# An encoder layer on one core: one loop over the feature groups for both requests, activations streamed from DRAM, f16 output projection

## The chip, the cores and the metric

One core of a Trainium2 chip runs the whole kernel in one launch. The metric is the device time of that launch in microseconds; lower is better.

## The reference, cut to what matters

Two requests, a prompt of 2048 tokens ("p") and a sample of 512 ("s"), go through one layer with the same weights:

```python
shift, scale, gate = split(silu(c) @ w_ada + b_ada, 3)
h = rmsnorm(x, g_pre) * (1 + scale) + shift
[qa ka va ga | qb kb vb gb] = h @ w_in          # 1024 -> 4096
ya = dilated_mixture(rope(qa), rope(ka), va) * silu(ga)   # 8 heads, windows (128,1) (512,4) (2048,16)
yb = diff_attention(rope(qb), rope(kb), vb) * silu(gb)    # 4 heads, two softmax maps, dense over the request
y = concat(ya, yb) @ w_out                      # 1024 -> 1024
out = x + gate * rmsnorm(y, g_post)
```

Everything is float32 with a tight tolerance, so each float32 product is made of three f16 products of a high and a low half (high by high, high by low, low by high); in the output projection the halves are of the 32-bit type that the trace shows as f32.

## The kernel before, in words

The 1024 mixed features are eight groups of 128: groups 4 to 7 are the four heads of B, groups 0 to 3 are four pairs of heads of A. Tokens are taken in superblocks of 512: the prompt has four, the sample one. For a group and a superblock there are four pieces of work: `kv_proj` (L421, matmuls in L433), `qg_proj` (queries in L508, gate in L529), the attention items (`ItemB`, L549, or `ItemA`, L661), and the write of the result to DRAM (L654, L757). A group of B has four items in a superblock, a group of A eight.

An item of B makes scores (L571, L577) in PSUM, a maximum on VectorE (L579), its negative on GpSimd (L582), the exponential on ScalarE (L587), the difference of the two maps and its high and low halves (L604, L606, L614), turns these by DMA transposes (L607, L615) and multiplies with the values (L626). An item of A makes scores of two kinds: for the two wide windows in four 32-column groups of the array (L681), and for the narrow window with all 128 columns at once (L686). For that second form `qg_proj` copies the queries of A into another order (L538). It then adds masks, takes maxima (L691, L693), exponentials (L700), halves (L715, L717), transposes (L718, L719), and multiplies (L735, L741).

**Order of the work.** `units` (L902) is a list of 16: first the sample with the eight groups in `ORDER` (4, 0, 5, 1, 6, 2, 7, 3), then the prompt with the same eight. The loop at L928 goes over units and over their superblocks. In each turn `interleave` (L884) mixes the attention items ("main") with projections that are needed next ("fill"), by estimated costs; the tile framework then places the instructions on the engines' queues in an order of its own, by a model of time. Queues are in order. All DMAs, transposes among them, are issued by SyncE (SP).

In the sample's eight units the weights of a group are loaded (`raw_load`, L160), scaled by their largest entry (`raw_split`, L257: L264 and a reduction over partitions on GpSimd, L272), split into halves (L286, L287), used, and also written to DRAM (L289). The prompt's units load the halves from there (`load_w`, L291). In the sample's last units the prompt's activations h are made too (`make_h`, L343); all four superblocks then stay in SBUF. PSUM is dealt out anew at L930: while the sample is worked on, scores are 512 wide in 3 banks, 3 banks for projections, 2 for the rest; after it three score tiles of two banks each, one bank for projections, one for the rest.

The output projection (`out_proj`, L819) reads y of one 128-token tile, splits it (L827, L829), makes 48 matmuls of 512 columns (L845), a mean square (L850), and adds x (L852, L853). There are 20 tiles; 16 are given as fill to the last superblock of the last unit, with a factor of 0.1 on their cost (`LF`, L997) that puts nearly all of them behind it, 4 come after (L999).

Of the kernel before, what the change touches and what calls it, by code (L numbers as in the profile page):

```python
# [8 lines left out]
F32 = mybir.dt.float32  # L9
# [19 lines left out]
LF = 0.1  # L29
PPB, HLB, ATB, SCB, PJB, PVB = 5, 4, 3, 3, 1, 1  # L30
PSI = 0
SSC, SPJ, SPV = 3, 3, 2
HSU = ((0,), (), (1,), (2,), (3,))
AQ = 1
WOA = [4, 1]
# [6 lines left out]
def hybrid_kernel(ctx, tc, x_p, x_s, w_in, w_ada, w_out, cvec, cols, lamv, gsub,  # L42
# [11 lines left out]
    CPM = SMAX // 4 + 32  # L54
# [11 lines left out]
    wp = stack_wp.enter_context(tc.tile_pool(name="wp", bufs=3))  # L66
# [3 lines left out]
    def psum(sw, sc, pj, pv):  # L70
        """deal the banks of PSUM out to scores (sw floats wide), projections and the rest"""
# [10 lines left out]
    psum(512, SSC, SPJ, SPV)  # L82
# [29 lines left out]
    cols_sb = C([P, 42], F32, "cols")        # b_ada, g_pre, g_post, feature 128 k + p at [p, k]; row sums  # L112
# [11 lines left out]
    # DRAM scratch  # L124
    w_spill = {g: dr.tile([P, 2, KT, 2, 256], F16, tag=f"wsp{g}", name=f"wsp{g}") for g in range(8)}
# [25 lines left out]
    def pow2(e_out, inv_out, src, name):  # L151
        """e_out: the power of two at or below src (>= 1e-30); inv_out: 2 / e_out."""
# [4 lines left out]

    RAW = {}

    def raw_load(n):  # L160
        raw = T(big, [P, KT, 512], F32, f"hT{1 + n % 2}")
        nc.sync.dma_start(raw, w_in[ORDER[n]])
        RAW[n] = raw

# [12 lines left out]
    def ada(ps, wa, scp, b0):  # L177
        """ps[:, b0 + q, :] = 128 columns of silu(c) @ w_ada on the partitions, from 512 columns wa of w_ada"""
# [13 lines left out]
    def modulation():  # L192
# [3 lines left out]
        for n, slot in enumerate(("hT2", "hT3", None, "hT0")):  # L196
            if slot:
                t = T(big, [P, KT, 512], F32, slot)
                halves = t[:, 0:4], t[:, 4:8]
            else:  # L200
                halves = [T(kv, [P, KT // 2, 512], F32, "K") for _ in range(2)]
# [8 lines left out]
        for r in "sp":  # L210
# [8 lines left out]
            g3 = T(tn, [P, 2], F32, "g3")  # L219
            nc.gpsimd.partition_all_reduce(g3, g2, channels=P, reduce_op=bass.bass_isa.ReduceOp.max)  # L220
            G = T(tn, [P, 1], F32, "G")
            V.tensor_add(G, g3[:, 0:1], g3[:, 1:2])
            E = T(tn, [P, 1], F32, "E")
            S = T(tn, [P, 1], F32, "S")
            pow2(E, S, G, f"h{r}")
# [5 lines left out]
    gcol = C([P, KT, 2], F32, "gcol")        # gate * g_post  # L231

    def gate_half(n):
        wa = T(big, [P, KT, 512], F32, "hT3")
# [22 lines left out]
    def raw_split(n):  # L257
        """Scale and split w_in of the n-th group; keep a copy of the halves in DRAM."""
        g, raw = ORDER[n], RAW[n]
        mg = T(tn, [P, 1], F32, "mg")  # L260
        for q in range(0, KT, AQ):
            # one slot for the partial maxima: other work gets in between
            am = T(tn, [P, 1], F32, "am", bufs=1)
            V.tensor_reduce(am, raw[:, q:q + AQ, :].rearrange("p a b -> p (a b)"), axis=AX.X, op=ALU.max,  # L264
# [821 lines left out]
```

## Time and profile before

| | |
|---|---|
| median of 3 runs | 2204.32 us (2203.71 to 2205.79) |
| span of the profiled execution, first to last instruction | 2200.1 us; its own device time is not listed, and the span lies 4.2 us under the median of the runs |
| TensorE matmul busy | 1882.9 us (86%) |
| VectorE / ScalarE / GpSimd busy | 67% / 53% / 28% |
| DMA engines, mean busy share | 63.5%, 298 MB moved |
| mean granted TensorE clock | 0.953 of full speed |

Busy time of TensorE counts overlapping matmuls once. The stages differ, so they are read one by one: up to about 122 us the weights of the modulation and the first activations; up to 543 us the sample; up to 2012 us the prompt's attention; then the output projection. A write of y (L654, L757) ends each superblock of a group, and the stretches below are cut at these.

### The profile page before, as it was taken

What the parts mean: (1) busy time and instruction counts of PE and PEld (TensorE: products, weight loads), DVE (VectorE), ACT (ScalarE), POOL (GpSimd) and SP (SyncE); (2) the same over time, 40 slices, a digit from 0 to 9 for tenths busy, and PEclk for the clock granted to TensorE, in tenths of its full rate; (3) what the DMA queues carried; (4) which work ended last, traced back from release to release, by engine and by line L of the source; (5) the groups of instructions that cost most, each with busy time, mean ns of one, the idle gap of its engine ahead of it and who ended that gap; (6) DMA issues with size and microseconds to landing.
All of it is one profiled execution on the core that took longest, in us unless ns stands there. A gap on an engine that the chain in (4) does not pass through costs nothing. (4 is left out here: it accounts for less than half of the span.)

```text
span 2200.1 us, 45341 instructions
## 1 busy us (share of the span) xinstructions
PE 1882.9 (86%) x17537; PEld 1327.6 (60%) x17537; DVE 1471.3 (67%) x3047; ACT 1172.2 (53%) x2298; POOL 623.5 (28%) x1422
## 2 busy tenths in 40 slices
PE   3657777898888989898899998889998888879998
PEld 1434655675555567565666665556765565548886
DVE  2545667576788766787776587877567887765443
ACT  3224456785666655566665465666556666642111
POOL 1222343352332322233332223333222323211000
PEclk9777988999999999999999999999999999979999
DMA  8263765865566667557767845677755566897442
GB/s 351 95 193 80 199 173 136 187 134 109 101 117 125 119 119 130 121 104 118 139 105 127 154 90 101 121 141 121 135 118 102 101 107 121 155 193 185 148 146 95
DMA packets 705431, 297.82 MB, mean 135 GB/s; under 512 B 636976, under 2 KB 681792, under 8 KB 698816
## 3 DMA queue, kind: packets, MB, share of 16 engines
q1 hardware_dynamic: 705216, 294.94, 63.1%
q8 instruction: 137, 2.24, 0.4%
q14 instruction: 78, 0.64, 0.1%
HBM read 96.37 MB, written 43.26 MB: 63 GB/s over the span
## 5 line engine op out<-in xcount | busy, mean ns | idle before, releaser
L433 PE MATMUL pj<-w,hT 128*128 128x256 f16 x3840 | 468.6, 277 | 15.2 <-DVE sg L534 6.1
L433 PEld LDWEIGHTS <-hT 128*128 128x128 f16 x3840 | 374.0, 99 | 82.5 <-issue 24.5
L587 ACT ACTIVATE pp<-sc,nb,us 128x1024 f32<-128x1024 f32 (+1 forms) x288 | 330.3, 1150 | 155.7 <-POOL nb L582 155.6
L579 DVE TENSOR_REDUCE mx<-sc 128x1 f32<-128x1024 f32 (+1 forms) x288 | 331.0, 1159 | 75.5 <-PE sc L577 75.0
L508 PE MATMUL pj<-w,hT 128*128 128x128 f16 x3840 | 255.5, 225 | 20.7 <-ACT q L514 20.0
L508 PEld LDWEIGHTS <-hT 128*128 128x128 f16 x3840 | 233.7, 101 | 42.8 <-issue 38.5
L626 PE MATMUL pv<-V,at 128*128 128x128 f16 x3264 | 228.5, 225 | 35.4 <-DMA at<-hl 33.9
L571 PE MATMUL sc<-K,Qc 128*128 128x512 f16 x544 | 170.4, 389 | 99.2 <-ACT pp L587 95.6
L626 PEld LDWEIGHTS <-at 128*128 128x128 f16 x3264 | 199.6, 101 | 67.5 <-DMA at<-hl 43.6
L529 PE MATMUL pj<-hT,w 128*128 128x512 f16 x960 | 229.3, 386 | 12.9 <-ACT q L514 9.6
L416 POOL TENSOR_TENSOR rp<-q,tab_sb 128x64 f32<-128x64 f32 x160 | 75.0, 469 | 471.4 <-ACT q L439 295.9
L717 DVE SCALAR_TENSOR_TENSOR hl<-pp,Z,hl 128x640 f16<-128x640 f32 (+2 forms) x160 | 141.7, 887 | 99.7 <-DMA at<-hl 60.7
L715 ACT ACTIVATE hl<-pp,Z 128x640 f16<-128x640 f32 (+2 forms) x160 | 131.4, 824 | 136.2 <-DMA at<-hl 87.8
L700 ACT ACTIVATE pp<-pp,nb,us 128x640 f32<-128x640 f32 (+2 forms) x160 | 146.4, 915 | 69.7 <-POOL nb L697 69.4
L614 DVE SCALAR_TENSOR_TENSOR hl<-pp,rz,hl 128x1024 f16<-128x1024 f32 (+1 forms) x144 | 173.6, 1223 | 9.6 <-ACT hl L606 7.6
L845 PE MATMUL sc<-hT,yh 128*128 128x512 f32 x480 | 165.2, 397 | 10.5 <-DVE yh L827 5.8
L604 DVE SCALAR_TENSOR_TENSOR pp<-pp,rz,pp 128x1024 f32<-128x1024 f32 (+1 forms) x144 | 171.1, 1225 | 2.1
L606 ACT ACTIVATE hl<-pp,rz 128x1024 f16<-128x1024 f32 (+1 forms) x144 | 155.2, 1093 | 30.6 <-issue 26.6
L529 PEld LDWEIGHTS <-w 128*128 128x128 f16 x960 | 91.5, 99 | 124.5 <-issue 30.1
L697 POOL TENSOR_SCALAR nb<-mx,us 128x1 f32<-128x1 f32 x160 | 100.2, 627 | 205.1 <-DVE mx L693 123.4
L582 POOL TENSOR_SCALAR nb<-mx,us 128x1 f32<-128x1 f32 x160 | 89.2, 557 | 204.6 <-DVE mx L579 173.0
L681 PE MATMUL sc<-K,Qc 128*32 128x384 f16 (+2 forms) x1280 | 120.4, 340 | 17.9 <-DVE Qc L538 12.7
(162 smaller groups left out, 2774.7 us busy)
## 6 DMA issues: line engine op xcount, KB each, us to landing
hT<-in_w_in_dram SPq DMA_DIRECT2D x8, 2048.0 KB, 10.6
wsp<-w SPq DMA_DIRECT2D x16, 1024.0 KB, 4.8
pp<-in_x_p_dram SPq DMA_DIRECT2D x32, 512.0 KB, 5.1
w<-wsp SPq DMA_DIRECT2D x16, 1024.0 KB, 5.8
out_dram<-pp SPq DMA_DIRECT2D x20, 512.0 KB, 3.0
at<-hl SPq DMA_TRANSPOSE x608, 3.2
yp<-yt SPq DMA_DIRECT2D x32, 256.0 KB, 2.4
y<-yp SPq DMA_DIRECT2D x16, 512.0 KB, 4.1
```

The costliest lines, as they stand in the source:

```text
L433: mm(ps[:, jj, :], lhsT=hT[:, a, k, j * P:(j + 1) * P], rhs=w[:, k, b, :], start=(k == 0 and i == 0), stop=(k == KT - 1 and i == 2))
L508: mm(ps[:, jj, 0:128], lhsT=hT[:, a, k, j * P:(j + 1) * P], rhs=w[:, k, b, 0:128], start=(k == 0 and i == 0), stop=(k == KT - 1 and i == 2))
L529: mm(ps, lhsT=w[:, k, b, 128:256], rhs=hT[:, a, k, :], start=(k == 0 and i == 0), stop=(k == KT - 1 and i == 2))
L571: mm(ps[:, n * 512:(n + 1) * 512], lhsT=Qc[:, j, m, 0, :], rhs=K[:, t:t + 4, m, :], start=True, stop=False)
L579: V.reduce_max(mx[:, hf:hf + 1], ps[:, :HW], axis=AX.X)
L587: act(pt[m, hf][:, :HW], pss[hf][:, :HW], AF.Exp, scale=u["sc"], bias=nb, accum_out=Z[:, 2 * m + hf:2 * m + hf + 1])
L604: V.scalar_tensor_tensor(a, a, rz[:, 2:3], pt[0, hf][:, :HW], op0=ALU.mult, op1=ALU.add)
L606: act(hi[:, :HW], a, AF.Copy, scale=rz[:, 3:4])
L614: V.scalar_tensor_tensor(lo[:, :HW], a, sg, hi, op0=ALU.mult, op1=ALU.subtract)
L626: mm(po[:, :128], lhsT=a[:, k, :], rhs=Vv[:, k, 128 * b:128 * b + 128], start=(k == 0 and i == 0), stop=(k == NT - 1 and i == 2))
L700: act(sb[:, :NA], sb[:, :NA], AF.Exp, scale=u["sc"], bias=nb, accum_out=Z[:, 0:1])
L845: mm(ps[:, 512 * h:512 * h + 512], lhsT=a[:, k, :], rhs=b, start=(k == 0 and i == 0), stop=(k == KT - 1 and i == 2))
```

## The change

The two passes become one. For each of the eight groups (now in the order 0, 4, 1, 5, 2, 6, 3, 7, so A comes first and a group of B last) the loop goes over five superblocks: the prompt's four, then the sample's. A group's weights are scaled and split once and used for both requests; they are not written to DRAM.

- The activations h of all five superblocks are made before the loop, written to DRAM, and read back for every group: two buffers of 2 MB, each read in four DMAs (`load_h`).
- Keys and values of p and s have buffers of their own; narrow-window values (`load_v1`) are read superblock by superblock; one mask buffer for each request.
- Maxima over partitions (`allmax`) are made by a transpose on TensorE, a VectorE maximum and a matmul with ones, in place of GpSimd's reduction.
- Narrow-window scores of A also go in four 32-column groups, without the copy of the queries.
- Every write of y is preceded by a VectorE maximum (`y_out`). The output projection scales y and `w_out` by powers of two and uses f16 halves; the high half of y is made on ScalarE.
- In the last group, output tiles of the superblock before the last one are fill: 12 of 20 tiles; 8 come after the loop.
- PSUM is dealt out in the second way (three double score tiles, one, one) for the whole loop.

The core of the diff; lines that are only "..." are left out:

```diff
-PPB, HLB, ATB, SCB, PJB, PVB = 5, 4, 3, 3, 1, 1
...
-ORDER = (4, 0, 5, 1, 6, 2, 7, 3)
+PPB, HLB, ATB, WPB, HB = 5, 4, 3, 4, 2
+ORDER = (0, 4, 1, 5, 2, 6, 3, 7)
...
+    def allmax(col, tag="pv"):
+        tp = PT([P, 512], tag)
+        nc.tensor.transpose(tp[0:1, 0:P], col, id_sb)
+        m = T(tn, [1, 1], F32, "am1")
+        V.reduce_max(m, tp[0:1, 0:P], axis=AX.X)
+        bc = PT([P, 512], tag)
+        mm(bc[:, 0:1], lhsT=one_sb, rhs=m, start=True, stop=True)
+        return bc[:, 0:1]
...
+    def load_h(r, c):
+        hT = T(big, [P, 2, KT, 512], F16, "h", bufs=HB)
+        for q in range(4):
+            nc.sync.dma_start(hT[:, q // 2, 4 * (q % 2):4 * (q % 2) + 4, :],
+                              h_dram[r, c][:, q // 2, 4 * (q % 2):4 * (q % 2) + 4, :])
         HT[r, c] = hT
...
-        if g < 4:
-            Qr = T(qp, [P, 2, 2, 4, P], F16, "Qc", bufs=3)
-            for j in range(4):
-                V.tensor_copy(
...
+    def y_out(r, g, c, y):
+        V.tensor_reduce(yam[:, c + (r == "s") * NSB["p"], g:g + 1], y, axis=AX.X, op=ALU.max,
+                        apply_absolute_value=True)
+        nc.sync.dma_start(y_dram[r][c][:, g, :], y)
...
             for s in range(2):
-                mm(ps[:, m1], lhsT=Qc[:, h, s, bb, :], rhs=kw, start=s == 0, stop=s == 1)
+                for j in range(4):
+                    mm(ps[32 * j:32 * j + 32, m1], lhsT=Qc[:, j, h, s, 32 * bb:32 * bb + 32], rhs=kw,
+                       start=s == 0, stop=s == 1)
...
+    def y_first(r, c, j):
+        if j == 0:
+            y_scale(r, c)
...
+        act(yh, y32, AF.Copy, scale=s[:, 1:2])
+        V.scalar_tensor_tensor(yl, y32, s[:, 1:2], yh, op0=ALU.mult, op1=ALU.subtract)
...
+    prev = ("p", 0)
+    for n, (r, c) in enumerate(SBS):
+        work = [kv_proj(r, g0, c)]
+        if n == 0:
+            work.append(qg_proj(r, g0, c))
+        if n == 2:
+            work.append(raw_scale(1))
+        if n == 3:
+            work += [raw_split(1, 1), raw_split(1, 0)]
+        if n + 1 < NS:
+            interleave(make_h(*SBS[n + 1]), 6.4, chain(*work), 11 * len(work))
...
+    psum(1024, 3, 1, 1)
+    for n, g in enumerate(ORDER):
+        g2 = ORDER[n + 1] if n + 1 < NU else None
+        for i, (r, c) in enumerate(SBS):
+            fl, fc = [], 0.01
+            side = iter(())
+            if n + 1 < NU or i + 2 < NS:
+                load_h(*SBS[(i + 2) % NS])
+            if i == 0 and n + 2 < NU:
+                raw_load(n + 2)
+            if n + 2 < NU:
+                if i == 1:
+                    side = raw_scale(n + 2)
+                elif i == 2:
+                    side = raw_split(n + 2, 1)
+                elif i == 4:
+                    side = raw_split(n + 2, 0)
...
+            r2, c2 = SBS[(i + 1) % NS]
+            if i + 1 < NS:
+                fl.append(qg_proj(r2, g, c2))
...
+            if g2 is not None:
+                fl.append(kv_proj(r2, g2, c2))
...
+            if g2 is None and i >= 2:
+                tiles = [(*SBS[i - 2], j) for j in range(4)]
+                fl.append(out_proj(tiles))
...
+            interleave(main, mc, weave(chain(*fl), side), fc, LEAD[2 * (r == "p") + (g < 4)])
+    run(out_proj([(*SBS[k], j) for k in (-2, -1) for j in range(4)]))
```

## Rows read from the trace of the kernel before

**Rows 1.** The page, part 1: TensorE's busy time and instructions.

```profile
PE 1882.9 (86%) x17537; PEld 1327.6 (60%) x17537; DVE 1471.3 (67%) x3047; ACT 1172.2 (53%) x2298; POOL 623.5 (28%) x1422
```

**Rows 2.** Windows by stage: stretch, length, busy us of each engine, clock, DMA, GB/s.

```profile
0.00:122.00 122.00, 64.89 (x496) 41.45 (x497) 49.12 (x137) 34.16 (x60) 20.93 (x60) 0.90 0.61 232
122.00:543.00 421.00, 326.88 (x2989) 237.89 (x2987) 263.57 (x721) 239.64 (x582) 155.95 (x365) 0.88 0.62 148
543.00:2012.00 1469.00, 1311.37 (x13263) 899.69 (x13263) 1085.26 (x2109) 879.47 (x1622) 437.27 (x981) 0.97 0.67 124
2012.00:2200.00 188.00, 179.73 (x793) 148.59 (x792) 73.39 (x82) 18.95 (x34) 9.31 (x17) 0.98 0.43 133
```

**Rows 3.** Windows of one prompt unit of B, then one of A (same columns).

```profile
907.00:1142.00 235.00, 209.47 (x2038) 138.41 (x2038) 187.24 (x300) 150.98 (x286) 78.32 (x170) 0.97 0.64 116
1142.00:1275.00 133.00, 125.96 (x1406) 92.43 (x1403) 81.89 (x234) 73.37 (x131) 34.55 (x88) 0.99 0.73 130
```

**Rows 4.** Windows of one sample unit of A, then one of B (columns as before).

```profile
413.00:449.00 36.00, 31.84 (x324) 24.48 (x322) 25.77 (x72) 27.49 (x67) 14.99 (x33) 0.95 0.90 196
449.00:494.00 45.00, 40.71 (x393) 35.40 (x392) 30.72 (x76) 37.27 (x106) 22.31 (x44) 1.00 0.57 120
```

**Rows 5.** Groups of instructions: the projections' matmuls of the whole span.

```profile
L433 PE MATMUL pj<-w,hT 128*128 128x256 f16 x3840 | 468.6, 277 | 15.2 <-DVE sg L534 6.1 <-DVE hT L403 4.7 <-ACT hT L401 3.6
L508 PE MATMUL pj<-w,hT 128*128 128x128 f16 x3840 | 255.5, 225 | 20.7 <-ACT q L514 20.0 <-DVE sg L534 0.5
L529 PE MATMUL pj<-hT,w 128*128 128x512 f16 x960 | 229.3, 386 | 12.9 <-ACT q L514 9.6 <-DVE S L105 2.9 <-DVE V L449 0.2
```

**Rows 6.** Waits, longest in total: TensorE for a free score tile.

```profile
PE sc L571 <- ACT pp L587: 95.6, 85, 11.1
```

**Rows 7.** Windows: the 12 us behind each of 12 weight loads (1 MB, 652 to 1614 us), summed.

```profile
sum 144.00, PE 128.11 PEld 96.22 DVE 89.85 ACT 71.97 POOL 35.14; mean PE 10.68 PEld 8.02 DVE 7.49 ACT 6.00 POOL 2.93
```

**Rows 8.** Line L615, 707 to 709.5 us: two transposes issued behind such a load.

```profile
L615 SPq DMA_TRANSPOSE at<-hl x2: 1337/2722/4106, 707.8 to 709.2; - x2
...
DMA to landing us min/median/max: 6.7/7.2/7.6
```

**Rows 9.** DMA issues: size in KB, median us from issue to landing.

```profile
hT<-in_w_in_dram SPq DMA_DIRECT2D x8, 2048.0 KB, 10.6
...
at<-hl SPq DMA_TRANSPOSE x608, 3.2
```

**Rows 10.** Groups of instructions: VectorE's work on a group's weights.

```profile
L287 DVE SCALAR_TENSOR_TENSOR w<-hT,S,w 128x512 f16<-128x512 f32 x64 | 45.4, 747 | 0.0
L264 DVE TENSOR_REDUCE am<-hT 128x1 f32<-128x512 f32 x64 | 43.6, 681 | 26.0 <-POOL mg L269 18.0 <-POOL mg L267 4.7 <-DMA hT<-in_w_in_dram 3.0
```

**Rows 11.** Timeline of TensorE: wide and narrow scores of an item, twice (start, us).

```profile
334.57 0.30 PE L681 MATMUL sc<-K,Qc 128*32 128x128 f16 x8
334.80 0.39 PE L686 MATMUL sc<-K,Qc 128*128 128x256 f16 x2
...
1163.47 0.62 PE L681 MATMUL sc<-K,Qc 128*32 128x512 f16 x8
1164.02 0.39 PE L686 MATMUL sc<-K,Qc 128*128 128x256 f16 x2
1164.25 0.22 PE L508 MATMUL pj<-w,hT 128*128 128x128 f16 x1
```

**Rows 12.** A window inside the output projection; the chain's piece of f16 gate matmuls.

```profile
2050.00:2100.00 50.00, 50.00 (x223) 41.42 (x222) 22.47 (x25) 5.57 (x10) 2.74 (x5) 1.00 0.45 138
...
1890.77 5.34 PE pj L529 x24
```

**Rows 13.** Line L718: SP's time to issue a transpose (ns, min/median/max).

```profile
L718 SPq DMA_TRANSPOSE at<-hl x160: 1177/1227/3237, 182.6 to 2000.6; - x160
```

**Rows 14.** Timeline of TensorE: the first projection and the first scores.

```profile
63.15 1.04 PE L433 MATMUL pj<-w,hT 128*128 128x256 f16 x4 [3.56 <-ACT hT L401]
...
122.69 0.38 PE L571 MATMUL sc<-K,Qc 128*128 128x512 f16 x1
```

More of the change, by code (lines that the diff above doesn't have):

```diff
@@ L390, in first_h, with make_h @@
             smul(xt, xt, rsqrt_mean(ss, 1.0 / D))
+            xs.append(xt)
+            yield 0.05
+        XN[r, c] = xs
+    XN = {}
+    def make_h(r, c):
+        yield from norm_x(r, c)
+        xs = XN[r, c]
+        hT = T(big, [P, 2, KT, 512], F16, "h", bufs=HB)
+        HT[r, c] = hT
+        for k in range(KT):
+            tp = PT([P, 4, P], "sc")
+            for j in range(4):
+                nc.tensor.transpose(tp[:, j, :], xs[j][:, k * P:(k + 1) * P], id_sb)
+            yield 0.7
+            h32 = T(hl, [P, 512], F32, "hl")
+            act(h32, tp, AF.Identity, scale=gs[r][:, k:k + 1], bias=sh[r][:, k:k + 1])
+            V.tensor_copy(hT[:, 0, k, :], h32)
+            V.tensor_sub(hT[:, 1, k, :], h32, hT[:, 0, k, :])
+            yield 0.05
+        spill_h(r, c)
+    def first_h(r):
+        for _ in norm_x(r, 0):
+            pass
+        xs = XN[r, 0]
+        xT = [T(kv, [P, 4, 512], F32, "V") for _ in range(2)]
+        for j in range(4):
             for h in range(2):
@@ L403, in first_h @@
             V.tensor_sub(hT[:, 1, k, :], xk, hT[:, 0, k, :])
+        spill_h(r, 0)
         yield
@@ L791, in hybrid_kernel, with wo_scale @@
     WO = {}
+    wo = {}
+    def wo_scale():
+        mg = T(tn, [P, 8], F32, "mg")
+        for q in range(4):
+            raw = T(wp, [P, 2, D], F32, "w")
+            nc.sync.dma_start(raw, w_out[:, 2 * q:2 * q + 2, :])
+            for i in range(2):
+                V.tensor_reduce(mg[:, 2 * q + i:2 * q + i + 1], raw[:, i, :], axis=AX.X, op=ALU.max,
+                                apply_absolute_value=True)
+                yield 0.0
+        ag = T(tn, [P, 1], F32, "ag")
+        V.reduce_max(ag, mg, axis=AX.X)
+        E = T(tn, [P, 1], F32, "E")
+        wo["S"] = C([P, 1], F32, "woS")
+        wo["i"] = C([P, 1], F32, "woi")
+        pow2(E, wo["S"], allmax(ag), "wo")
+        smul(wo["i"], E, 2.0 ** -13 * 2.0 ** -13)
+        smul(wo["S"], wo["S"], 2.0 ** 12)
+        yield 0.0
@@ L808, in hybrid_kernel @@
+        WO[n] = [(hi[:, k, :], lo[:, k, :]) for k in range(KT)]
     GG = {}
-    TL = []
     def load_gg():
-        gt = T(big, [P, 2, D], F32, "hT0")
+        gt = T(wp, [P, 2, D], F32, "w")
         for r in "ps":
@@ L835, in out_proj @@
             yh, yl = nxt
-            if n + 1 < len(tiles):
-                nxt = first(*tiles[n + 1])
+            s = YS[r, c]
             xt = T(pp, [P, D], F32, "pp")
@@ L847, in out_proj @@
                     yield 0.65
+                    if h == 0 and k == 0 and n + 1 < len(tiles):
+                        nxt = y_first(*tiles[n + 1])
             jk = T(pp, [P, D], F32, "pp")
@@ L901, in hybrid_kernel @@
     assert NSB["s"] == 1
-    units = [("s", g) for g in ORDER] + [("p", g) for g in ORDER]
-    NU = len(units)
-    h0 = first_h("s")
+    SBS = [("p", c) for c in range(NSB["p"])] + [("s", 0)]
+    NS = len(SBS)
+    NU = len(ORDER)
+    g0 = ORDER[0]
+    h0 = first_h("p")
     next(h0)
-    raw_load(0)
     md = modulation()
     next(md)
-    raw_load(1)
-    run(raw_split(0))
+    raw_load(0)
+    run(raw_scale(0))
     run(md)
+    for i in (1, 0):
+        run(raw_split(0, i))
     next(h0)
-    new_unit(*units[0])
-    unit_scalars(*units[0])
-    run(kv_proj("s", ORDER[0], 0))
-    run(qg_proj("s", ORDER[0], 0))
+    for r in "ps":
+        new_unit(r, g0)
+        unit_scalars(r, g0)
     zt = T(ev, [16, 4, 256], F16, "tq")
     nc.gpsimd.memset(zt, 0.0)
-    for r in "sp":
+    for r in "ps":
         for i in range(2):
@@ L996, in hybrid_kernel @@
                 mc = MCA[r == "p"] * 8 * (0.53 * SQ[r] / 2048 + 0.22) + 2 * (0.11 * SQ[r] / 128 + 0.9)
-            interleave(main, mc, chain(*fl), fc * (LF if i + 1 == NU and last else 1),
-                       LEAD[2 * (r == "p") + (g < 4)])
-    run(out_proj([("p", NSB["p"] - 1, j) for j in range(4)]))
+            interleave(main, mc, weave(chain(*fl), side), fc, LEAD[2 * (r == "p") + (g < 4)])
+    run(out_proj([(*SBS[k], j) for k in (-2, -1) for j in range(4)]))
 _ARGS = ("x_p", "x_s", "w_in", "w_ada", "w_out", "cvec", "cols", "lamv", "gsub",
```

335 lines of the change are left out of this document (133 added, 202 removed).

## The prediction

> **What bounds the kernel now.** I first read the page's busy times, then cut the span into stages, since one share hides four different limits. TensorE is busy 1882.9 of 2200.1 us [rows 1], and it is the engine to follow in every stage, but what it waits for changes. Up to 122 us it is busy 64.9 us: weights and activations arrive, and the first scores start at 122.69 us [rows 2, 14]. From 122 to 543 us, the sample's pass, it is busy 326.9 of 421 us, at a granted clock of 0.88 [rows 2], that is, partly at the lower of its two levels (1.2 and 2.4 GHz). From 543 to 2012 us, the prompt's pass, it is busy 1311.4 of 1469 us, which is 89.3%, at 0.97 [rows 2]. In the last 188 us it is busy 179.7 [rows 2]. So the idle time lies at 57 us before the first scores, 94 in the sample's pass, 158 in the prompt's and 8 at the end.
>
> Inside the prompt's pass a unit of B takes 235 us with TensorE at 89% and VectorE at 80%, and a unit of A 133 us with TensorE at 95% and VectorE at 62% [rows 3]. In B the largest single wait of TensorE is for a score tile that ScalarE's exponential frees, 95.6 us in 85 waits [rows 6]. That path runs over VectorE's maximum, so VectorE's load matters there although it is not full.
>
> **The change, part by part, as a sum over the new order.**
>
> *Before the loop.* The first projection starts at 63 us [rows 14]; its inputs (modulation, one superblock, one group's weights) are the same, so I keep that. Keys, values, queries and gate of one group and superblock cost TensorE 468.6 + 255.5 + 229.3 over 40, or 23.8 us, of which 11.7 is keys and values [rows 5]. The first superblock takes 24. Then three more h are made beside 11.7 us of projection each. No row shows that alone; the lower bound is 12, where h is hidden, and the upper 25, from two sample units that each held one prompt superblock's h and took 36 and 45 us for some 30 us of their own work [rows 4], so 6 to 15 on top. I take 20 each, 60. The second group's weights add 8 maxima of 0.681 and 8 halves of 0.747 us, 11.4 us of VectorE [rows 10]; half of it shown is about 5. The last keys and values have no cover, 12. Dealing out PSUM anew and the first item's latency: 8, between 0 and 15. Together 172 us, where the kernel before needs 123.
>
> *One pair of groups (B and A) in the loop.* The prompt's part is 235 + 133 = 368 us [rows 3]. On it come:
> - The sample's two turns. The sample's pair of units took 81 us with TensorE at 72.6 [rows 4], but that holds the transposes of two prompt superblocks. A turn alone is 23.8 of projection and some 7 of attention (an estimate: in B 16 score matmuls at 0.215 and 48 of 128 columns at a quarter of that), about 30.5. At 89.3% it takes 34, a pair 68. Bounds are 61, no gap at all, and 81, as it stood. SP does not set it: a sample turn of A issues some 22 transposes at 1.23 us [rows 13] and 9 plain DMAs at about 0.5, 31 us.
> - Reading h: ten loads of 2 MB a pair. The near row is the kernel's own reload of weights, 1 MB each. In the 12 us behind each of the twelve TensorE is busy 10.68, or 89.0%, against 89.3% in the stage [rows 2, 7], so on average they cost nothing, though the two transposes behind one of them landed after 6.7 and 7.6 us where 3.2 is usual [rows 8, 9]. The bounds for 2 MB are 0 and 4.0 us, the latter if that delay were fully idle time. I take 1, nearest to rows 7, so 10, less 1 for the two weight loads that go.
> - VectorE: two groups' weights, 22.9 us, and ten maxima of y at 0.681, 6.8, less 20 copies of queries of about 0.25, 5: some 25 more, with two maxima over partitions by TensorE and back. They fall on turns where VectorE is at 62 to 80%. Bounds 0 and 25; I take 8.
> - Narrow scores in column groups. Eight 32-column matmuls take 0.23 us at 128 columns and 0.55 at 512 [rows 11], so 0.34 at 256, against 0.23 for the two full ones (1164.02 to 1164.25). They now follow matmuls of their own form, so the 0.12 of fixed time is paid once and not twice. That leaves a difference of about nothing, bounds plus and minus 0.1 on 80 items a pair.
>
> A pair is then 368 + 68 + 9 + 8 = 453 us, and three pairs 1359.
>
> The Trainium skill (TensorEngine Tiling (Array Packing), sections Key Properties and Restrictions) speaks against that last edit: changing the tiling mode drains the engine, and column tiling gives up the fast weight load. By this rule alone, 0.11 more an item and 160 items, the sum would be 18 us higher. The fixed 0.12 us in the rows agrees with a drain.
>
> *The fourth pair.* A: 133 + 34 + 5 for loads + 8 for the gate and the scaling of the output weights, 180. B is last, without the next group's keys and values, but with 12 output tiles. A f16 matmul of 512 columns starts every (5.34 - 0.39) / 23 = 0.215 us, where the f32 form needs 50 / 223 = 0.224 [rows 12]; a tile of 48 is 10.35 us instead of 10.8. The first two superblocks have little fill and follow VectorE, 187.2 / 4 = 46.8 [rows 3], so 50 each. The next two have TensorE's 209.5 / 4 = 52.4, less 11.7, plus 41.4 for four tiles, 82; I take 84, as the output tiles also hold a score tile each, which sharpens the wait of rows 6. The sample's turn: 8 of attention and 41.4, with gaps 52. With 3 for loads: 323 us.
>
> *The end.* Eight tiles, 83 us, 8 for the last tile's norm and write as now (188 less 179.7) [rows 2], 3 for the scale of y: 94.
>
> Sum: 172 + 1359 + 180 + 323 + 94 = 2128 us, against a span of 2200.1. The span lies 4.2 us under the median of the runs, 2204.32, so the time is 2132 us. Where the gain comes from, in the same terms: the sample's pass and the start shrink from 543 to 172 + 4 x 68 = 444 (99), twelve of twenty tiles now fill TensorE's gaps in the last B group (about 55), and loads, VectorE and others give back about 80.
>
> At nothing I cost the high half of y on ScalarE, which is busy 19 of the last 188 us [rows 2], and GpSimd's reductions, which leave a queue that is at 28% [rows 1]; if ScalarE were late, each tile would wait about 1 us, 8 at the end.
>
> What is late next is VectorE in B's turns, and SP in the sample's turns of A.
>
> **Rivals.**
>
> *The streamed h holds up the transposes; slower.* The place is the DMA engines, and SP's queue ahead of them. A load waits on SP until the buffer's last reader, a projection of the turn before, has run; the transposes of attention weights issued after it stand behind that wait, and then behind 2 MB that needs 10.6 us to land [rows 9]. TensorE waits for these transposes. For: the landing of 6.7 and 7.6 us [rows 8], and a DMA share of 0.73 in A and 0.90 in a sample turn [rows 3, 4], before 80 MB more are read. Against: rows 7. With 39 loads it decides the sign from 3.0 us each (2132 + 39 x 2 = 2210). At the full 4.0 the time is 2132 + 39 x 3 = 2249. Chance 0.23. The Trainium skill (DMA: Bandwidth & Descriptors, section Queues, rings and completion order) says that each DMA engine consumes one issuing engine's descriptors in ring order, which would put every transpose behind the whole load. The 6.7 and 7.6 us agree.
>
> *The loop fills better; about 2076.* The sample's turns bring more projections than attention, and TensorE could reach 92% in place of 89.3%. Its work in the loop up to the last group is about 1539 x 0.893 = 1374; at 92% that is 1494, 45 less, and with free loads 11 less again. For: A is at 95% already [rows 3]. Against: one bank for projections, where the sample's pass had three. Chance 0.20.
>
> *VectorE takes it back; no change.* All 25 us a pair on the path, 51 in three pairs, and a start of 195: 2132 + 51 + 23 = 2206. Chance 0.07: B stands at 80%, A does not.
>
> **How the numbers follow.** My sum holds with 0.50. About 0.2% (4 us) is what a measurement of this kernel can tell from no change. Faster has the forecast and the second rival, 0.70; the third rival is no change, 0.07; slower is the first, 0.23. The range reaches down to 2060 (the better loop, with the start at 155) and up to 2240 (most of the first rival), which leaves about one in ten on each side.
>
> **What would show it.** First scores at 165 to 180 us; a pair of groups in 440 to 465 us; the last group 310 to 330; 94 us behind it. Right on loads: transposes landing late without TensorE waiting longer for them in sum. Wrong: TensorE's share in the loop under 86% with waits for transposes at the top means the first rival; VectorE over 85% in B means the third; first scores beyond 200 us would mean that the making of h was not covered.

## The result, and the profile after

The changed kernel takes 2281.41 us, median of 4 runs (2278.94 to 2282.70), beside 2204.02 for the kernel before: a ratio of 1.037, 95% interval 1.034 to 1.040. It is slower where 2132 us and faster were forecast. The profiled execution has a span of 2280.1 us.

The page's first part, after (see [rows 1]):

```profile
PE 1896.0 (83%) x18545; PEld 1291.5 (57%) x18545; DVE 1491.4 (65%) x3084; ACT 1191.5 (52%) x2238; POOL 533.1 (23%) x1369
```

No engine has more work than before worth the name (TensorE 13 us, VectorE 20); TensorE only stands idle for 384 us in place of 317. To see where, the span is cut at the last write of y of a group: the start, three pairs of A and B, the fourth A, the last B, the end. Windows after (columns as in [rows 2]):

```profile
0.00:175.00 175.00, 124.97 (x1030) 95.29 (x1030) 105.77 (x280) 86.17 (x156) 33.82 (x88) 0.86 0.73 253
175.00:653.00 478.00, 404.23 (x4362) 288.82 (x4365) 333.17 (x700) 268.44 (x515) 125.32 (x324) 0.95 0.72 154
653.00:1136.00 483.00, 414.90 (x4449) 295.67 (x4450) 338.14 (x728) 278.96 (x535) 129.53 (x334) 0.95 0.73 152
1136.00:1615.00 479.00, 407.32 (x4305) 290.13 (x4308) 334.62 (x690) 269.91 (x517) 121.62 (x325) 0.95 0.75 164
1615.00:1794.00 179.00, 145.87 (x1816) 112.31 (x1809) 103.57 (x317) 93.49 (x174) 40.02 (x102) 0.93 0.82 169
1794.00:2179.00 385.00, 310.79 (x2208) 170.13 (x2205) 238.42 (x321) 176.63 (x319) 76.90 (x180) 0.90 0.53 125
2179.00:2280.00 101.00, 87.87 (x390) 39.17 (x389) 37.69 (x51) 17.88 (x24) 5.90 (x16) 0.92 0.34 121
```

Set against the terms of the sum (the fourth column is run e2 below, which leaves out reading h):

| term | forecast | after | e2 |
|---|---|---|---|
| start | 172 | 175 | 175 |
| three pairs | 1359 | 1440 | 1397 |
| fourth A | 180 | 179 | 176 |
| last B with 12 tiles | 323 | 385 | 368 |
| end | 94 | 101 | 100 |
| span | 2128 | 2280 | 2216 |

So 152 us were missed, 81 of them in the pairs and 62 in the last group. In a pair TensorE is busy 409 us on average, where 335 for the prompt [rows 3] and 61 for the sample's turns were reckoned, so 12 of 27 us are busy time; the clock is 0.95, where the prompt's pass had 0.97. In the last group the forecast's terms hold 295 us of busy time (four times 52.4 less 11.7, 124 of tiles, 8 of the sample's attention) in 323; it is 311 in 385. There 16 of the 62 us are busy time, some 6 of them a gate that falls behind the cut, and 46 are idle time.

What TensorE waits for, first in the kernel before, then after (engine, line, what it waits for; us in total, times, longest):

```profile
PE pv L626 <- DMA at<-hl: 33.9, 35, 5.6
PE pv L735 <- DMA at<-hl: 12.8, 15, 2.9
```

```profile
PE sc L576 <- ACT pp L592: 69.9, 69, 10.1
PE pv L631 <- DMA at<-hl: 67.2, 38, 9.8
PE pv L742 <- DMA at<-hl: 44.6, 31, 3.9
```

The wait for a free score tile fell from 95.6 us [rows 6] to 69.9, and the waits for transposes grew from 47 to 112, of which 33 fall in the last group.

### The profile page after: what moved, and what is told of

Read it like the earlier page. It is cut to its first block, busy times and chain, and to the rows that moved or that the text cites. A ratio compares the mean times of both kernels' runs of the same rounds, so it can differ in the third digit from the quotient of the medians.

```text
span 2280.1 us, 47414 instructions
## 1 busy us (share of the span) xinstructions
PE 1896.0 (83%) x18545; PEld 1291.5 (57%) x18545; DVE 1491.4 (65%) x3084; ACT 1191.5 (52%) x2238; POOL 533.1 (23%) x1369
## 5 line engine op out<-in xcount | busy, mean ns | idle before, releaser
L439 PE MATMUL pj<-w,h 128*128 128x256 f16 x3840 | 480.9, 283 | 33.0 <-DVE sg L539 11.4
L439 PEld LDWEIGHTS <-h 128*128 128x128 f16 x3840 | 382.0, 102 | 110.4 <-issue 46.9
L631 PEld LDWEIGHTS <-at 128*128 128x128 f16 x3264 | 209.7, 104 | 118.4 <-DMA at<-hl 84.0
L513 PE MATMUL pj<-w,h 128*128 128x128 f16 x3840 | 246.1, 222 | 14.6 <-ACT q L519 6.6
L534 PE MATMUL pj<-h,w 128*128 128x512 f16 x960 | 230.8, 395 | 22.8 <-ACT q L519 22.8
L513 PEld LDWEIGHTS <-h 128*128 128x128 f16 x3840 | 227.1, 100 | 37.9 <-issue 33.6
L576 PE MATMUL sc<-K,Qc 128*128 128x512 f16 x512 | 160.3, 393 | 65.2 <-ACT pp L592 64.8
L422 POOL TENSOR_TENSOR rp<-q,tab_sb 128x64 f32<-128x64 f32 x160 | 68.9, 431 | 598.3 <-ACT q L445 408.1
L611 ACT ACTIVATE hl<-pp,rz 128x1024 f16<-128x1024 f32 (+1 forms) x144 | 156.1, 1096 | 67.6 <-issue 50.9
L534 PEld LDWEIGHTS <-w 128*128 128x128 f16 x960 | 94.5, 101 | 140.3 <-issue 48.2
L889 PEld LDWEIGHTS <-w 128*128 128x128 f16 x960 | 94.5, 99 | 118.0 <-issue 8.9
L587 POOL TENSOR_SCALAR nb<-mx,us 128x1 f32<-128x1 f32 x160 | 87.4, 547 | 266.1 <-DVE mx L584 245.9
L704 POOL TENSOR_SCALAR nb<-mx,us 128x1 f32<-128x1 f32 x160 | 74.3, 465 | 211.6 <-DVE mx L700 169.8
L889 PE MATMUL sc<-raw,w 128*128 128x512 f16 x480 | 112.9, 392 | 4.0 <-ACT pp L592 3.2
```

What stands on the lines that cost most here:

```text
L439: mm(ps[:, jj, :], lhsT=hT[:, a, k, j * P:(j + 1) * P], rhs=w[:, k, b, :], start=(k == 0 and i == 0), stop=(k == KT - 1 and i == 2))
L513: mm(ps[:, jj, 0:128], lhsT=hT[:, a, k, j * P:(j + 1) * P], rhs=w[:, k, b, 0:128], start=(k == 0 and i == 0), stop=(k == KT - 1 and i == 2))
L534: mm(ps, lhsT=w[:, k, b, 128:256], rhs=hT[:, a, k, :], start=(k == 0 and i == 0), stop=(k == KT - 1 and i == 2))
L576: mm(ps[:, n * 512:(n + 1) * 512], lhsT=Qc[:, j, m, 0, :], rhs=K[:, t:t + 4, m, :], start=True, stop=False)
L611: act(hi[:, :HW], a, AF.Copy, scale=rz[:, 3:4])
L631: mm(po[:, :128], lhsT=a[:, k, :], rhs=Vv[:, k, 128 * b:128 * b + 128], start=(k == 0 and i == 0), stop=(k == NT - 1 and i == 2))
```

## The experiments

Line numbers in the waits of an experiment can differ by a few from those of the changed kernel. All ratios are to the kernel before, with 95% intervals.

**e2: no reading of h.** In place of the load, the two superblocks of h made last are used in turn, so every group's work has its size but not its data.

```diff
     def load_h(r, c):
-        hT = T(big, [P, 2, KT, 512], F16, "h", bufs=HB)
-        for q in range(4):
-            nc.sync.dma_start(hT[...], h_dram[r, c][...])
-        HT[r, c] = hT
+        if not KEEP:
+            KEEP.extend([HT["p", NSB["p"] - 1], HT["s", 0]])
+        KEEP.append(KEEP.pop(0))
+        HT[r, c] = KEEP[0]
```

> The loop reads no h back from DRAM: its projections use the two superblocks of h made last, in turn, so what is left out is the reading of h. Everything else is as in the changed kernel. Theory B (the 39 loads of 2 MB cost the 27 us by which each of the first three pairs of groups overran the sum): a pair falls from 480 us to about 453, and the time to about 2190 us. Rival (VectorE's added work, the single projection bank, the order of the work): a pair stays above 470, the time above 2250 us.

2216.78 us, ratio 1.006 (1.005 to 1.008): reading h costs 65 us, and without it the loop is still not faster. Windows and waits of e2:

```profile
175.00:649.00 474.00, 411.38 (x4445) 290.58 (x4444) 339.58 (x732) 278.27 (x534) 137.59 (x333) 0.96 0.56 109
649.00:1103.00 454.00, 397.37 (x4314) 286.40 (x4314) 327.59 (x691) 269.75 (x515) 131.68 (x324) 0.95 0.58 111
1103.00:1572.00 469.00, 412.43 (x4482) 295.95 (x4484) 339.58 (x719) 276.43 (x529) 138.39 (x333) 0.97 0.62 126
1572.00:1748.00 176.00, 151.03 (x1852) 116.02 (x1847) 104.35 (x312) 94.66 (x176) 41.96 (x106) 0.94 0.65 123
1748.00:2116.00 368.00, 300.26 (x2082) 162.41 (x2079) 232.46 (x313) 171.38 (x310) 79.13 (x171) 0.88 0.48 112
```

```profile
PE sc L577 <- ACT pp L593: 60.5, 67, 6.3
PE pv L743 <- DMA at<-hl: 40.2, 26, 4.5
PE pv L632 <- DMA at<-hl: 38.3, 28, 4.9
```

A pair is 466 us on average, TensorE busy 407 of it: its work is the same, and 13 us of idle time are gone. Some 43 of the 65 us show in two waits of TensorE, for transposes (112 to 78) and for score tiles (70 to 61). Waits for h itself are 5 us in all. In the changed kernel the line of the load has these rows (who waited for it, and the time to landing):

```profile
  POOL rp L422: 2.1, 1
  PEld L513: 1.6, 1
  PE pj L513: 1.3, 1
DMA to landing us min/median/max: 3.6/5.6/9.7
```

**Where the load is issued: e3, e10, e14.** e3 issues the four DMAs of a load from GpSimd's queue; e10 cuts a load into 16 pieces and puts them between the steps of the fill; e14 is e2 with the same bytes moved from DRAM to DRAM, on which nothing waits (like e2 it leaves out the use of h).

```diff
-            nc.sync.dma_start(hT[...], h_dram[r, c][...])
+            nc.gpsimd.dma_start(hT[...], h_dram[r, c][...])
...
+        for q in range(16):
+            nc.sync.dma_start(hT[:, q // 8, q % 8, :], h_dram[r, c][:, q // 8, q % 8, :])
+            yield 0.0
+            yield 0.0
...
+            nc.sync.dma_start(to[...], h_dram[r, c][...])
```

> The loads of h are issued by GpSimd instead of SP; the bytes are the same. If the loads cost by standing ahead of the transposes in SP's queue or in SP's rings, most of what the run without loads gains comes back: about 2210 us. If they cost by the DMA engines' time alone, the time stays within 20 us of the changed kernel's 2281. If GpSimd's own small operations are late behind its DMA issues, it gets longer than 2281.

> Each load of h goes in 16 pieces of 128 KB, woven one by one into the turn's projections, instead of four pieces of 512 KB at its start; the bytes are the same. Theory B1 (the 65 us that the loads cost come from transposes that stand behind a 2 MB burst): two thirds come back, about 2240 us. Rival B2 (the DMA engines' time and SP's issue time): no gain, or worse, as 12 more issues a turn at some 0.5 us go through SP, which is 0.84 busy in A: 2280 to 2330 us.

> As the run without loads (projections use the two superblocks of h made last), but the same 39 times four DMAs of 512 KB are issued on SP at the same places, from DRAM to another place in DRAM, so that nothing waits for them and they wait for no buffer of SBUF. If the loads cost by the DMA engines' time and the transposes behind them, the time is near the changed kernel's, 2260 to 2285. If they cost by waits for the buffer on SP, or by projections that wait for h, it is near the run without loads, 2217 to 2230.

e3 takes 2411.11 us (1.097, 1.092 to 1.102), e10 2293.19 (1.041, 1.038 to 1.043). GpSimd makes the negative maximum ahead of every exponential, and now stands in its queue waiting until a buffer of h is free:

```profile
L350 POOL DMA_DIRECT2D h<-hp x124 | 68.3, 556 | 85.3 <-PE pj L439 47.7 <-PE pj L534 28.6 <-PE sc L692 5.1
```

So a wait ahead of a load is dear where exponentials stand behind it, and of the two queues SP, as in the change, is the better place. Smaller pieces don't help. They do what they were meant to: of the 608 transposes of attention weights one in ten took longer than 6.0 us from issue to landing in the changed kernel, than 4.2 in e10, and than 4.2 in e2 without any load. But SP now spends 1542 us on issuing DMAs in place of 1356, summed over its DMA instructions, and TensorE's waits for the transposes of queries grow from 13 to 35 us. e14 (2387.16 us; 1.081, 1.077 to 1.085) tells nothing on this: with nothing to wait for, its copies all ran in the first group, which took 385 us at a DMA share of 0.95; the groups after it ran as in e2, but for the second, 25 us shorter.

**e1: no tiles in the last group.** All 20 tiles come after the loop.

```diff
-            if g2 is None and i >= 2:
-                tiles = [(*SBS[i - 2], j) for j in range(4)]
-                fl.append(out_proj(tiles))
-                fc += 11 * len(tiles)
...
-    run(out_proj([(*SBS[k], j) for k in (-2, -1) for j in range(4)]))
+    run(out_proj([(*SBS[k], j) for k in range(NS) for j in range(4)]))
```

> All 20 output tiles run behind the loop; the last group has its queries, gate and attention alone. Theory A (the 12 tiles in the last B group disturb its attention): the last group falls from 385 us to about 256, the stretch behind it grows from 101 to about 218, so the time is 2270 us or a little less. Rival (the tiles fill gaps of TensorE there, as the prediction had it, and the last group is long for another reason): the tiles cost 57 us more behind the loop than in it, so 2320 us or more.

2274.49 us (1.034, 1.029 to 1.038): the 12 tiles can leave the last group without loss. The last group of e1:

```profile
1792.00:2045.00 253.00, 187.64 (x1628) 113.10 (x1624) 189.77 (x252) 150.68 (x283) 68.20 (x156) 0.86 0.58 120
```

Without tiles TensorE idles 65 of 253 us, with them 74 of 385. In sum the 123 us of tiles filled nothing; they were simply added. What TensorE waits for did change. Its longest waits in the last group, in e1 and then in the changed kernel:

```profile
PE sc L576 <- ACT pp L592: 27.6, 21, 4.1
PE pv L652 <- ACT o L650: 23.6, 12, 3.2
PE pv L631 <- DMA at<-hl: 6.2, 6, 2.4
```

```profile
PE pv L631 <- DMA at<-hl: 33.1, 13, 9.8
PE pv L652 <- ACT o L650: 11.3, 5, 3.4
PE sc L576 <- ACT pp L592: 11.1, 11, 2.4
```

So the tiles cover some 29 us of the old waits for ScalarE and bring 27 us of new ones for transposes. The timeline of TensorE in the changed kernel's last group shows how, and below it that of ScalarE:

```profile
1949.69 1.06 PE L889 MATMUL sc<-raw,w 128*128 128x512 f16 x2
...
1967.20 0.39 PE L582 MATMUL sc<-K,Qc 64*128 64x512 f16 x2
1977.35 1.03 PE L631 MATMUL pv<-V,at 128*128 128x128 f16 x8 [9.75 <-DMA at<-hl]
...
1982.92 1.66 PE L631 MATMUL pv<-V,at 128*128 128x128 f16 x24
1986.10 5.34 PE L889 MATMUL sc<-raw,w 128*128 128x512 f16 x24 [1.52 <-ACT pp L592]
...
1996.45 5.34 PE L889 MATMUL sc<-raw,w 128*128 128x512 f16 x24
...
2006.82 3.40 PE L889 MATMUL sc<-raw,w 128*128 128x512 f16 x15
```

```profile
1971.64 1.15 ACT L872 ACTIVATE w<-w,ys 128x1024 f16<-128x1024 f32 x1 [5.49 <-DMA w<-yp]
1972.69 2.18 ACT L611 ACTIVATE hl<-pp,rz 128x1024 f16<-128x1024 f32 x2
...
2007.02 1.02 ACT L896 ACTIVATE pp<-sc 128x1024 f32<-128x1024 f32 x1 [9.25 <-PE sc L889]
```

The first tile is mixed with attention up to 1967; then TensorE waits 9.75 us for a transpose with no tile to hand. In that time ScalarE stands 5.49 us before the high half of the next tile's y (L872), which is not read yet, and the high half of attention's weights (L611), which the transpose needs, comes behind it. Then three tiles run one behind the other on TensorE, 10.35 us apart, with hardly a matmul of attention between them, and ScalarE waits 9.25 us for the end of the second (L896), and as long for the third. Queues are in order, so the order decided beforehand puts work where there was no gap and none where there is one.

**What could hold the tiles back: e4, e6, e7, e11.** A tile reads y through a buffer that the tile before frees (e4 reads from GpSimd's queue, e11 two tiles ahead into the buffers of h), sits in a score tile (e6 uses the projections' bank), and takes two buffers that attention uses (e7 gives it others).

```diff
-        nc.sync.dma_start(y32..., y_dram[r][c][:, :, P * j:P * j + P])
+            nc.gpsimd.dma_start(y32...[:, 4 * q:4 * q + 4, :], y_dram[r][c][:, 4 * q:4 * q + 4, ...])
...
-            ps = PT([P, PS["w"]], "sc")
+                ps = PT([P, 512], "pj")
...
-            xt = T(pp, [P, D], F32, "pp")
+            xt = T(qp, [P, D], F32, "maskp", bufs=1)
-            jk = T(pp, [P, D], F32, "pp")
+            jk = y32
...
-        t = T(wp, [P, 8 * D], mybir.dt.uint8, "w")
+            YB[r, c] = T(big, [P, 16 * D], mybir.dt.uint8, "h", bufs=HB)
```

> The output projection's reads of y are issued by GpSimd, in two halves, instead of SP. In the changed kernel SP stands 61 us in the last group before these reads, which wait for a buffer, with attention's transposes behind them. Theory A1 (that wait on SP is what makes the last group long): TensorE's 33 us of waits for transposes there go, the last group falls from 385 to about 345 us, the time to about 2240. Rival A2 (the tiles take one of the three score tiles, or two of the five buffers of the exponentials): the last group stays above 370 us and the time within 15 us of 2281.

> Output tiles accumulate in two halves of 512 columns in the projections' PSUM bank instead of one of the three score tiles; each half is copied out by ScalarE. Theory A2 (a tile that is woven into attention holds a score tile for 25 us and leaves B two): the last group falls from 384 to about 330 us and the time to about 2230. Rival (buffers of the exponentials, or SP): the last group stays above 370; the stretch behind it may grow by 10 to 20 us, since one bank must be emptied before the next half.

> x and the normalised rows of an output tile no longer take two of the five buffers that the exponentials of B use four of per item; they lie in the buffer of the masks and in the tile's own dead input. Theory A3 (these buffers hold up the exponentials): the last group falls from 384 to about 330 us, the time to about 2230. Rival (the score tile): the last group stays above 370 and the time within 10 us of 2281.

> y of the output tiles is read two tiles ahead into the two buffers of h, which are free by then, instead of the four shared weight buffers. In the changed kernel SP stands before a read of y until a tile's matmuls free a buffer, and ScalarE stands behind that read with the high half of y, with attention's exponentials and halves behind it; TensorE then idles up to 9.8 us and afterwards runs three tiles in a row. Theory A4 (these two waits are why the tiles fill nothing): the last group falls from 384 to about 340 us and the time to about 2235. Rival A5 (TensorE takes tiles in blocks because of the order the framework gives, whatever the buffers): the last group stays above 365, the time above 2260 us.

e4 2302.05 us (1.045, 1.043 to 1.046), e6 2299.53 (1.043, 1.040 to 1.046), e7 2273.80 (1.032, 1.028 to 1.035), e11 2275.89 (1.031, 1.028 to 1.035). None of them alone is what holds the tiles: two gain 6 to 8 us, two lose 18 to 21. The last group stays at 374 to 377 us in e6, e7 and e11, and takes 406 in e4. e6 has a price of its own, 15 us in which TensorE waits for its one bank. In e11, where y is there in time, TensorE still waits 19 us for transposes in the last group, and 18 for score tiles, which was 11.

**f2: A last.** The groups in the order that the kernel before has.

```diff
-ORDER = (0, 4, 1, 5, 2, 6, 3, 7)
+ORDER = (4, 0, 5, 1, 6, 2, 7, 3)
```

> The changed kernel with B first and A last in each pair of groups, as the kernel before had it; the last group is then one of A. Theory: the 74 us in which TensorE idles in the last group come from B's attention, which has no projections of a next group left and follows VectorE and ScalarE; in A they don't arise. Last A: about 180, less 58 of projections for a next group, plus 124 for 12 tiles, about 246, and the B group ahead of it 285, so 531 in place of 564: about 2250. Rival: the gaps come with the tiles themselves, which the queue holds in blocks of three, so the last group of A has them too: 2275 to 2290.

2260.7 us (1.028, 1.025 to 1.032), 21 us less. The last group, now A:

```profile
1876.00:2163.00 287.00, 239.36 (x1729) 122.78 (x1726) 134.32 (x336) 99.54 (x159) 32.02 (x76) 0.91 0.57 138
```

Idle time falls from 74 to 48 us, near the 31 to 44 of f2's other groups of A: much of it did belong to a B group that has no next group's projections. But 21 us came where 31 were expected, and TensorE is busy for 239 us. The tiles' matmuls keep it busy for 152 us, where in the changed kernel's last group it is 130, and the scores in column groups for 53, where it is 36 in that kernel's fourth A (times in which both run count twice). The last section shows why.

**Narrow scores and maxima: e9, e12.** e9 makes the narrow scores with all 128 columns again, from a small copy of the queries for each item; e12 leaves out the maxima of y (a constant stands in) and seven of eight of the weights'.

```diff
+            qr = T(ev, [P, 2, 4, 32], F16, "qr", bufs=3)
+            V.tensor_copy(qr, Qc[:, :, h, :, 32 * bb:32 * bb + 32].rearrange("p j s i -> p s j i"))
...
-                for j in range(4):
-                    mm(ps[32 * j:32 * j + 32, m1], lhsT=Qc[:, j, h, s, 32 * bb:32 * bb + 32], rhs=kw,
-                       start=s == 0, stop=s == 1)
+                mm(ps[:, m1], lhsT=qr[:, s].rearrange("p j i -> p (j i)"), rhs=kw, start=s == 0, stop=s == 1)
...
-        V.tensor_reduce(yam[:, c + (r == "s") * NSB["p"], g:g + 1], y, axis=AX.X, op=ALU.max,
-                        apply_absolute_value=True)
+    nc.gpsimd.memset(yam, 65536.0)
```

> Narrow scores of A again by two matmuls over all 128 columns, with a small VectorE copy per item of the queries (160 copies, some 0.23 us each) in place of the copies that the change dropped. If column groups cost 0.11 us an item on TensorE as the rows of single runs said, this saves at most 18 us where TensorE is the bound: 2263. If TensorE is not the bound in A's turns, the copies cost as much as it saves: 2275 to 2290.

> Left out: the maxima of y (a constant in their place) and seven of the eight maxima of each group's weights, so some 40 + 56 VectorE operations of 0.68 us, 65 us of VectorE in all; about 55 of it in the loop. Theory C (VectorE's added work is on the path in the pairs): 25 to 40 us less, 2245 us. Rival (it lies beside TensorE's work): within 10 us of 2281.

e9 takes 2268.72 us (1.030, 1.026 to 1.034), e12 2278.88 (1.034, 1.030 to 1.038). The maxima cost next to nothing: 2.5 us, within the intervals. For the narrow scores, the groups of instructions of the kernel before, of the changed one (two rows: prompt and sample) and of e9:

```profile
L686 PE MATMUL sc<-K,Qc 128*128 128x256 f16 x320 | 66.6, 286 | 0.0
```

```profile
L692 PE MATMUL sc<-K,Qc 128*32 128x256 f16 x1024 | 74.4, 279 | 0.0
L692 PE MATMUL sc<-Ks,Qc 128*32 128x256 f16 x256 | 12.8, 282 | 0.0
```

```profile
L693 PE MATMUL sc<-K,qr 128*128 128x256 f16 x256 | 49.3, 280 | 0.2 <-DVE qr L691 0.2
L693 PE MATMUL sc<-Ks,qr 128*128 128x256 f16 x64 | 12.8, 307 | 0.8 <-DVE qr L691 0.8
```

In column groups they keep TensorE busy 87.2 us, before 66.6, in e9 62.1. The 25 us between the last two are more than the 13 that the time gained, and the interval of that gain just touches the changed kernel's.

**Together: e13, f4, f5.** e13 is e9, e7 and e11 in one; f4 is f2 with e9; f5 is f4 with e2's edit.

> Three edits together: narrow scores over all 128 columns, y read ahead into the buffers of h, and x and the normalised rows out of the exponentials' buffers. If their effects add, and the first gives 13 us, the last 8 and the reads of y some 40, about 2220 us; if the tiles come in blocks whatever the buffers, about 2260. Neither theory puts it under the kernel before.

> As f2, and the narrow scores with all 128 columns as in e9. If the two act apart, 13 us under f2, about 2237 by the theory of f2; if e9's gain was a matter of the interval, the same as f2.

> As f4, and the activations are not read back, as in e2 (the loop uses the two superblocks made last). If loads, order of the groups and narrow scores are separate costs, 65 us under f4: about 2172, 1.5% under the kernel before, and the loop without its loads is then worth what was forecast to within 40 us. If they are one cost (idle time that one of them can take up for the other), it stays near e2: 2200 to 2215.

e13 2267.19 us (1.028, 1.025 to 1.031), where the three gains would add to 26 us and 14 came; f4 2266.99 (1.030, 1.027 to 1.033), no better than f2; f5 2211.09 (1.005, 1.003 to 1.007), 56 us under f4 but only 6 under e2. Loads are a cost of their own. The order of the groups, the narrow scores and the buffers don't add up: by these times each moves some of the same idle time.

**The f16 projection alone: f1, f6.** The kernel before with the maxima of y, scales and f16 halves, the tiles where they were. f6 finds the scale of the weights one unit earlier, with the changed kernel's maximum over partitions in place of GpSimd's.

```diff
+                y_out(r, g, c, st["tsb"])
...
-        hi = T(big, [P, KT, 512], F32R, ("hT3", "hT1")[n])
+        hi, lo = t[:, :, 0, :], t[:, :, 1, :]
+            act(hi[:, k:k + 2, :], raw, AF.Copy, scale=wo["S"])
...
+            act(yh, y32, AF.Copy, scale=s[:, 1:2])
...
+            if i + 2 == NU and c == 0:
+                fl.append(wo_scale())
```

> The kernel before with one part of the change alone: the f16 output projection (maxima of y before its writes, a power of two for y and for the output weights, f16 halves, the high half of y on ScalarE); loop, order and placing of the tiles stay. Theory: the tiles are TensorE's, 20 of them at 10.35 us in place of 10.8, and the maxima cost nothing as e12 showed, so 9 us less: about 2195. Rival: the last unit is a group of B at 80% VectorE, and the eight maxima of the output weights and the 40 of y go on its path: 2204 to 2215.

> As f1, but the scale of the output weights is found one unit earlier and the maxima over partitions go over TensorE, as the change has it, so that nothing in the last unit waits for a scale. In f1 the last unit took 191 us for 137, with VectorE waiting 32 us for GpSimd's reductions while scores waited for VectorE. If that is all of f1's loss, the last unit is 137 again and the f16 tiles save about 9: 2190 to 2200, faster than both kernels. If the f16 weights and maxima cost by themselves (VectorE, ScalarE, reads of the weights twice), 2215 to 2255.

f1 takes 2257.75 us (1.026, 1.023 to 1.029), f6 2240.36 (1.018, 1.016 to 1.021). The last unit of f1, and then of the kernel before:

```profile
1882.00:2073.00 191.00, 120.24 (x997) 67.12 (x997) 106.93 (x278) 75.97 (x114) 23.05 (x52) 0.79 0.68 152
```

```profile
1876.00:2013.00 137.00, 115.66 (x1001) 79.85 (x1000) 97.95 (x245) 62.91 (x103) 27.18 (x44) 0.90 0.92 185
```

The same work of TensorE, 54 us longer. The longest wait of TensorE there is for VectorE, which itself waits for GpSimd's reductions:

```profile
PE sc L688 <- DVE mx L700: 34.8, 8, 18.4
DVE p L154 <- POOL am L804: 32.4, 4, 14.1
```

In f6 that unit is back at 143 us, but the unit ahead, where the scale is found now, takes 247 for 234, and the prompt's units before it some 20 more together. The end gains nothing (190 us for 187), where f1 had gained 8 there (179). So in this form the f16 projection doesn't pay alone either. How much of that is the placing of its preparation was not taken further, and no version here beats the kernel before.

## Why the prediction was wrong

By the test that the prediction set (share under 86%, waits for transposes at the top) it is rival one: TensorE's share in the pairs is 85%, and the 112 us of waits for transposes stand above all others. But the test misleads. With the tiles out of the last group these waits are 71 us (e1), and reading h costs 65 us where the sum held 35 of it, so rival one's mechanism has some 30 of the 152 us. Without loads on both sides, e2 against the sum, 123 us stay: 65 in the three pairs, 48 in the last group, 10 elsewhere.

*What held.* The start: 175 for 172. The sample's turns, by the writes of y: 21 to 46 us each, the seven without tiles 226 together, or 32 on average where 34 was taken, and the last, with four tiles, 43 for 52. So by this cut the 99 us that the sample's pass was to give back did come back, and it is the prompt's turns that are longer. The price of a tile that runs by itself, 10.35 us. The fourth A, 179 for 180.

*"Twelve of twenty tiles now fill TensorE's gaps in the last B group (about 55)."* This step failed. The forecast had 323 us, 295 of them busy; it is 385 with 311. The profile before shows that gaps exist, not that tiles would stand in them: gaps last as long as one hand-off (9.75 us in the timeline), and the order on the queue is fixed beforehand. e1 shows it: with the tiles taken out, the idle time is the same to 9 us. With A last (f2) a third of it goes. The high half of y on ScalarE, which the sum put at nothing, does stand before attention's halves there, but with y read early (e11) the group is only some 8 us shorter. A single shared resource as the cause was sought and not found (e4, e6, e7, e11); that the order on TensorE's queue is the cause is read from the timeline, and no run changed it alone.

*Ten loads of h a pair at 1 us each.* The term was mis-sized: 39 loads cost 65 us (e2), 1.7 each. [Rows 7] gave the average behind twelve loads of 1 MB, in a kernel that moved 124 GB/s in that stage; here the pairs move 152 to 164. It is not the 3.0 a load from which on rival one alone would have decided the sign. Its mechanism is there: one transpose in ten lands after more than 6.0 us with the loads, and 4.2 without. The Trainium skill (DMA: Bandwidth & Descriptors, section Queues, rings and completion order) has each DMA engine consume descriptors in ring order, so that behind pieces of 128 KB a transpose should land sooner than behind a whole load; e10's trace agrees, with 4.2 us. But e10 is 12 us slower than the changed kernel all the same, so later landing is not shown to be what the 65 us are. How they divide between landing, SP's time and the waits that follow stays open.

*Three pairs of 453 us* held the prompt's part at the 368 us that it took before. Without loads a pair is 466 where 444 was reckoned. Of these 22 us about 11 are busy time: 5 are the narrow scores in column groups (20.6 us over four pairs, [rows 11] having been read as no difference); what the other 6 are no run shows, but matmuls take somewhat longer (those of keys and values 281 ns on average, 277 in [rows 5]) at a clock of 0.95 to 0.97. The other 11 are waits on several hand-offs, none of them large: transposes, queries, ScalarE. That share stays open. Of VectorE's 8 us the part of the maxima, over half of the work that came on, was not there (e12); the halves were not tried alone. VectorE is busy 77% of the changed kernel's B groups, not over 85%, so rival three falls.

*The narrow scores.* By the rule of the Trainium skill (TensorEngine Tiling (Array Packing), sections Key Properties and Restrictions) that a change of tiling mode drains the engine and that column tiling gives up the fast weight load, the sum would have had 18 us more; the rows give 20.6 over the kernel before and 25 over e9. The trace does not put this down to changes of mode: from 175 to 1615 us matmuls in column groups and others change places 210 times in the changed kernel and 287 times in e9. The forecast's 0 was wrong as busy time. As time it is 13 us in one place (e9) and nothing in another (f4).

*The end, 94,* was 101: TensorE is busy 88 us for 83, at a clock of 0.92 where the end had 0.98 [rows 2].

Rival two, the better loop, is out with TensorE at 85% in the pairs, not 92.

## What to carry to other kernels

Idle time in a profile is room only for work that the queue's order puts exactly there; before it is counted as filled, take the same work out and see whether the idle time changes. An average over a few transfers at a low DMA load is no price for many at a higher one: take the dearer end when the traffic rises by a quarter. A scale that must be known before the work starts (a maximum, a reduction, a power of two) is a wait on an in-order queue, and costs what stands behind it.

## What the runs showed that was not expected

TensorE's work is not its time here: e9 took 25 us of narrow scores off TensorE and the time moved by 13, and f4 by nothing.

A change between matmuls of column groups and full ones costs about 0.1 us each way. In f2's last group they alternate one by one (timeline of TensorE):

```profile
1962.22 0.39 PE L686 MATMUL sc<-K,Qc 128*32 128x512 f16 x1
1962.54 0.39 PE L889 MATMUL sc<-K,w 128*128 128x512 f16 x1
1962.86 0.39 PE L686 MATMUL sc<-K,Qc 128*32 128x512 f16 x1
```

From start to start it is 0.32 us, where full matmuls of 512 columns follow each other every 0.215; and the matmuls in column groups, of which eight take 0.55 to 0.61 us when they stand together, no longer run side by side there. In f2's last group column groups and other matmuls change places 206 times, in the changed kernel's fourth A 45 times; at 0.1 us each that is some 16 us (an estimate), about what the scores in column groups take longer there (17).

Idle time costs a second time, through the clock: the last group's 74 idle us go with a granted clock of 0.90 over 385 us, e2's 68 with 0.88, where the pairs have 0.95. In the changed kernel's records the clock is at its lower level (1.2 GHz) for about 306 us, before for 210, and in front of each of its 51 falls TensorE had stood idle. The gap of 9.75 us in the last group and the 8 us behind it (columns as in [rows 2]):

```profile
1968.00:1976.00 8.00, 0.00 (x0) 0.00 (x0) 6.78 (x7) 4.36 (x6) 0.36 (x1) 0.60 0.33 64
1976.00:1984.00 8.00, 6.66 (x49) 4.11 (x50) 2.69 (x3) 1.24 (x3) 0.00 (x0) 0.55 0.58 114
```

The matmuls behind the gap still run mostly at the lower level (0.55).
